# One pass over the k-tiles in the first FFN block, transposes moved into the next block, and FFN parts of 4, 4 and 3 blocks

## The chip, the core and the metric

The kernel runs on one core of a Trainium2 chip. The metric is the device time of one execution in microseconds (us); lower is better. Five engines run side by side, each taking its own instructions in order: TensorE (PE; its weight loads are listed as PEld), VectorE (DVE), ScalarE (ACT), GpSimd (POOL) and SyncE (SP), which here issues the transfers of the weights.

## What is computed

Two layers; in each a mixer of several attention-like heads, which the change does not touch, and then a SwiGLU block behind an RMS norm:

```python
def swiglu(h, w_gate, w_up, w_down):
    return (jax.nn.silu(h @ w_gate) * (h @ w_up)) @ w_down
...
for l in range(DEPTH):
    h = rms_norm(x, mix_norm_w[l])
    x = x + hybrid_mixer(h, ...)
    h = rms_norm(x, ffn_norm_w[l])
    x = x + swiglu(h, w_gate[l], w_up[l], w_down[l])
return rms_norm(x, final_norm_w)
```

x has 256 rows and 2048 columns, w_gate and w_up are 2048 x 5632, w_down is 5632 x 2048, all float32.

## The kernel before, in words

**Numbers.** Every float32 operand is split in a high part and a low part (`whi`, `wlo` of a weight; `hi`, `lo` of an activation). ACT makes the high part and DVE the low one, and a product is three matmuls: high by high, high by low, low by high. A weight comes from memory in units of 128 x 1024 (512 KB): `fetch` (L125) issues the transfer on SP into one of 3 buffers `raw`, `unit` (L140, L141) splits it into one of 4 buffer pairs `whi`, `wlo`. So DVE and ACT can be at most four units ahead of PE.

**Order.** The program is written through a framework that reorders instructions by its own model of the engines before it fixes the order on each queue; `tc.issue_after` (L70's log) only forbids a place before a given matmul. PSUM has eight banks: a pool of 4 (`dps`, tag "d", taken in rotation), `mg` with 2, `m0` and `m1` with one each (`mps`).

**FFN.** `ffn` works on blocks of 512 of the 5632 columns, 11 in all, and keeps x^T as 16 k-tiles `hl` (`hs`), high part and low part.

- The first block is `slow` (L923): all 16 k-tiles against w_gate into the two banks `pg`, then all 16 against w_up into `pu`, 96 matmuls each, on x^T that is not yet divided by the norm. Between the two, `norm.scale` gives the factor per row (`rstd`) and, through two small PE matmuls, the same along columns (`rb`). Behind both, `normalise` (L833) scales x^T in place, tile by tile: POOL adds high and low part (L841, `yn`), DVE multiplies by `rb` (L842), ACT and DVE split again into `hl` (L843, L844), POOL subtracts the two halves of the rows (L856, `dt`) and ACT and DVE split that (L829, L830, `sd`). Two pairs of tiles (3 and 4, 11 and 12) get three such combinations. A tile can only be overwritten when PE has read it for the last time.
- Every other block is `fast` (L893). With the sums in `sd` and combinations of the weights it computes gate and up together in 186 matmuls over seven PSUM banks `p1` to `p7` (`plain` 12 matmuls per k-tile, `quad` 21 per pair). At its end DVE and ACT put the banks together into `ga` (L915 to L921).
- Behind each block four PE transposes at a time (`hT`, 2 groups per block, L73) turn `ga`, and ACT and DVE split the result into `hid` (L951, L952), the left operand of the product with w_down.
- Blocks are gathered in parts, `FF_PARTS = (2, 2, 2, 2, 2, 1)`. After a part, `block_b` multiplies its `hid` with four column ranges of w_down (`dn`, two banks each), and `add_x` (L808) adds the result to x. In the last part `nxt.piece` starts on the following norm as each range is done; in the last layer this is `Final`, whose `last` (L310 and following) scales and stores one half of the rows after the other.

Of the kernel before, what the change touches and what calls it, by code (L numbers as in the profile page):

```python
# [20 lines left out]
P = 128  # L21
S = 256
# [1 line left out]
KT = D // P  # L24
DFF = 5632
FT = DFF // P
FF_PARTS = (2, 2, 2, 2, 2, 1)
PAIRS = (3, 11)
HM, HF, HG = 4, 8, 4
EPS = 1e-6  # L30
# [29 lines left out]
def tile_trunk(ctx: ExitStack, tc: tile.TileContext, x: bass.AP, wu: bass.AP, prm: bass.AP,  # L60
# [749 lines left out]
    def ffn(l, norm, nxt):  # L810
# [19 lines left out]
            dve.tensor_tensor(out=e[:, 1], in0=v, in1=f32(e[:, 0]), op=SUB)  # L830
            return e[:, 0], e[:, 1]

        def normalise(rb):  # L833

            free = [sd[i][:, j] for i in range(5) for j in range(4)]
            free = [v.rearrange("p (h x) -> p h x", h=2) if len(v.shape) == 2 else v for v in free]
            y = [None, None]
            for k in range(KT):
                hi, lo, hl = hs[k]
                y[k % 2] = yk = sp.tile([P, S], F32, tag="ac", name="yn", bufs=2)  # L840
                pool.tensor_tensor(out=yk, in0=f32(hi), in1=f32(lo), op=ADD)  # L841
                dve.tensor_tensor(out=yk, in0=yk, in1=rb, op=MUL)  # L842
                act.activation(out=hi, in_=yk, func=AF.Copy)  # L843
                dve.tensor_tensor(out=lo, in0=yk, in1=f32(hi), op=SUB)  # L844
                if k - 1 in PAIRS:
                    y0 = y[1 - k % 2]
                    st = sp.tile([P, 384], F32, tag="pt", name="st", bufs=2)
                    s1, s2, s4 = (st[:, i * P:(i + 1) * P] for i in range(3))
                    pool.tensor_tensor(out=s1, in0=y0[:, P:], in1=yk[:, P:], op=ADD)
                    pool.tensor_tensor(out=s2, in0=s1, in1=y0[:, :P], op=SUB)  # L850
                    pool.tensor_tensor(out=s4, in0=yk[:, :P], in1=s2, op=SUB)
                    for n, v in (("s1", s1), ("s2", s2), ("s4", s4)):
                        ops[n, k - 1] = hilo(free.pop(), v)
                else:
                    v = sp.tile([P, S], F32, tag="tz", name="dt", bufs=2)[:, :P]
                    pool.tensor_tensor(out=v, in0=yk[:, :P], in1=yk[:, P:], op=SUB)  # L856
                    ops["d", k] = hilo(free.pop(), v)

        def quad(c, k):

# [31 lines left out]

        def fast(c, first):  # L893

            ps = {3: dps("p3")}
            for i in ((1, 6, 7) if first else (2, 4, 5)):
                ps[i] = dps(f"p{i}")
            for i, tag in zip((2, 4, 5) if first else (6, 7, 1), ("mg", "mg", "m1")):
                ps[i] = mps(f"p{i}", tag)
            seen = set()  # L900
            for k in range(KT):
                if k - 1 in PAIRS:
                    continue
                for i, (ahi, alo), (whi, wlo) in quad(c, k) if k in PAIRS else plain(c, k):
                    end = k == KT - 1 or (i in (1, 6, 7) and k == PAIRS[-1])
                    pe.matmul(ps[i], ahi, whi, start=i not in seen, stop=False)
                    pe.matmul(ps[i], ahi, wlo, start=False, stop=False)
                    pe.matmul(ps[i], alo, whi, start=False, stop=end)
                    seen.add(i)
                if k == PAIRS[-1]:  # L910
                    act.copy(out=xs[:, 0], in_=ps[1])
                    dve.tensor_tensor(out=xs[:, 1], in0=ps[6], in1=xs[:, 0], op=ADD)
                    dve.tensor_tensor(out=ys[:, 0], in0=ps[7], in1=xs[:, 1], op=ADD)
# [7 lines left out]
                dve.tensor_tensor(out=ga[:, t], in0=ga[:, t], in1=ys[:, 1 - t], op=MUL)  # L921

        def slow(c):  # L923
            pg = [dps("pg") for t in range(2)]
            block_b(l, "gate", c, pg, hs, 0, KT, True, True)
            rstd, rb = norm.scale()
            for t in range(2):
                act.activation(out=ga[:, t], in_=pg[t], func=AF.Silu, scale=rstd[:, t:t + 1])
            pu = [dps("pu") for t in range(2)]
            block_b(l, "up", c, pu, hs, 0, KT, True, True)  # L930
            for t in range(2):
                dve.scalar_tensor_tensor(out=ga[:, t], in0=pu[t], scalar=rstd[:, t:t + 1], in1=ga[:, t],
                                         op0=MUL, op1=MUL)
            normalise(rb)

        for part, blocks in enumerate(FF_PARTS):
            nf = 4 * blocks
            fs = []
            for c in range(f0 * P, (f0 + nf) * P, 512):
                if c == 0:  # L940
                    slow(c)
                else:
                    fast(c, c == 512 or c == f0 * P)
                for q in range(0, 4, 2):
                    ps = mps("hT", "m0")
                    for i in range(2):
                        for t in range(2):
                            pe.transpose(ps[:, i * S + t * P:i * S + (t + 1) * P],
                                         ga[:, t, (q + i) * P:(q + i + 1) * P], ident)
                    hid = g4("hid", [2, 512], F32R, "gy")  # L950
                    act.copy(out=hid[:, 0], in_=ps)  # L951
                    dve.tensor_tensor(out=hid[:, 1], in0=ps, in1=f32(hid[:, 0]), op=SUB)  # L952
                    fs += [(hid[:, 0, i * S:(i + 1) * S], hid[:, 1, i * S:(i + 1) * S]) for i in range(2)]
            end = part == len(FF_PARTS) - 1
            for n in range(3 if end else 4):
                pst = [dps("dn") for t in range(2)]
                block_b(l, "down", n * 512, pst, fs, f0, nf, True, True)
                add_x(n, pst)
                if end:
                    nxt.piece(n)  # L960
# [97 lines left out]
```

## Time and profile before

| | |
|---|---|
| median of 3 runs | 2416.74 us (2416.14 to 2416.99) |
| the profiled execution, its own time | 2416.53 us |
| its span, first to last instruction | 2414.6 us |
| PE busy, share of the span | 98% |
| DVE, ACT, POOL busy | 70%, 50%, 12% |
| mean granted TensorE clock | 0.992 |
| first FFN block begins, layers 0 and 1 | 467.3 us, about 1663 us |
| HBM | 431.70 MB read, 180 GB/s over the span |

The 1.9 us between span and time lie around the profiled instructions. The profile puts busy time per engine, lists of waits and stretches of the execution side by side; a granted clock of 1.00 is 2.4 GHz for PE and 0.5 is 1.2 GHz.

### The profile page before, as it was taken

Reading aid. Unit: us, or ns where it says so; the run is one execution under the profiler, and the core shown is the slowest. Engines: PE = TensorE matmul, PEld = TensorE weight load, DVE = VectorE, ACT = ScalarE, POOL = GpSimd, SP = SyncE. Lnnn points to the kernel's source line nnn. Section 1 sums busy time; section 2 is a strip of 40 time slices with the busy share of each in tenths; the row PEclk is TensorE's granted clock in tenths of the full one; section 3 lists DMA queues with packets and bytes.
Section 4 is the critical chain, followed back from the end, with each engine's and each line's share of the span. In section 5 each row is a group of like instructions: output and inputs, shape, how many; then the busy total and the mean of one; then the engine's idle time right before and its main releaser. Section 6 shows DMA issues by size and latency. Waiting matters only on the chain.

```text
span 2414.6 us, 31866 instructions
## 1 busy us (share of the span) xinstructions
PE 2368.0 (98%) x11852; PEld 1995.4 (83%) x11852; DVE 1680.2 (70%) x2366; ACT 1212.0 (50%) x1783; POOL 278.3 (12%) x259
## 2 busy tenths in 40 slices
PE   9999999989999999999899999999999999999997
PEld 8888888867888888888798888888788888888886
DVE  5898655587676768576668976555866767676756
ACT  6754555554444444454466545555544444444443
POOL 0220000050101111010003000000501010111100
PEclk9999999999999999999999999999999999999998
DMA  6555455546565656665455554455465656565663
GB/s 218 167 174 175 138 166 176 176 166 198 175 210 191 200 185 200 191 198 183 151 169 175 175 163 152 155 186 192 148 200 191 201 169 213 192 196 186 203 203 114
DMA packets 120876, 435.89 MB, mean 181 GB/s; under 512 B 13584, under 2 KB 14480, under 8 KB 120720
## 3 DMA queue, kind: packets, MB, share of 16 engines
q1 hardware_dynamic: 120160, 432.70, 55.3%
q8 instruction: 93, 1.52, 0.3%
q10 hardware_dynamic: 560, 1.15, 0.1%
q14 instruction: 63, 0.52, 0.1%
HBM read 431.70 MB, written 2.10 MB: 180 GB/s over the span
## 4 chain that ended last, share of the span: by engine, by line
PE 88%; DVE 4%; issue 2%; ACT 2%; DMA 2%; POOL 1%; POOLq 0%; DVEq 0%; SPq 0%; ACTq 0%
PE p L70 31%; PE dn L70 19%; PE wo L70 7%; PE fq L70 4%; PE fk L70 4%; PE fv L70 4%; PE gkq L70 3%; PE mv L70 2%; DMA raw<-wu 2%; PE mq L70 2%; PE mk L70 2%; PE gvp L70 2%; PE gz L70 2%; PE pg L70 2%; DVE wlo L141 1%
## 5 line engine op out<-in xcount | busy, mean ns | idle before, releaser
L141 DVE TENSOR_TENSOR wlo<-raw,whi 128x1024 fp32r<-128x1024 f32 (+3 forms) x741 | 918.7, 1247 | 473.5 <-ACT whi L140 455.0
L140 ACT ACTIVATE whi<-raw 128x1024 fp32r<-128x1024 f32 (+3 forms) x741 | 775.8, 1053 | 772.2 <-PE dn L70 244.3
L70 PE MATMUL p<-whi,hl 128*128 128x512 f32 x1600 | 546.6, 391 | 1.0 <-ACT whi L140 1.0
L70 PE MATMUL dn<-whi,hid 128*128 128x512 f32 (+1 forms) x1440 | 444.3, 389 | 3.8 <-ACT hid L951 1.3
L70 PEld LDWEIGHTS p<-whi,hl 128*128 128x128 f32 x1600 | 301.3, 188 | 63.5 <-ACT whi L140 1.9
L70 PE MATMUL p<-wlo,hl 128*128 128x512 f32 x800 | 313.2, 392 | 7.1 <-DVE wlo L141 7.1
L70 PEld LDWEIGHTS dn<-whi,hid 128*128 128x128 f32 x1440 | 268.2, 189 | 60.0 <-ACT whi L140 3.0
L70 PE MATMUL dn<-wlo,hid 128*128 128x512 f32 (+1 forms) x720 | 277.2, 389 | 1.3 <-DVE wlo L141 1.3
L70 PE MATMUL p<-whi,sd 128*128 128x512 f32 x560 | 216.3, 391 | 0.0
L70 PEld LDWEIGHTS p<-wlo,hl 128*128 128x128 f32 x800 | 150.5, 188 | 41.0 <-DVE wlo L141 9.8
L874 POOL TENSOR_TENSOR rq<-rq 128x512 f32<-128x512 f32 x40 | 57.4, 1436 | 989.5 <-DVE rq L873 973.7
L70 PE MATMUL wo<-whi,yhl 128*128 128x512 f32 (+1 forms) x640 | 169.5, 351 | 0.0
L70 PEld LDWEIGHTS dn<-wlo,hid 128*128 128x128 f32 x720 | 136.5, 190 | 32.1 <-DVE wlo L141 5.2
L70 PEld LDWEIGHTS wo<-whi,yhl 128*128 128x128 f32 x640 | 112.6, 189 | 14.7
L70 PEld LDWEIGHTS p<-whi,sd 128*128 128x128 f32 x560 | 105.9, 189 | 21.6
L70 PE MATMUL wo<-wlo,yhl 128*128 128x512 f32 (+1 forms) x320 | 111.8, 349 | 0.0
L70 PE MATMUL p<-wlo,sd 128*128 128x512 f32 x280 | 109.8, 392 | 0.0
L878 ACT ACTIVATE th<-rq 128x1024 fp32r<-128x1024 f32 x80 | 84.0, 1050 | 43.8 <-POOL rq L876 27.8
L879 DVE TENSOR_TENSOR tl<-rq,th 128x1024 fp32r<-128x1024 f32 x80 | 99.8, 1248 | 3.5 <-ACT th L878 3.1
L876 POOL TENSOR_TENSOR rq<-rq 128x512 f32<-128x512 f32 x40 | 83.1, 2078 | 120.5 <-DVE rq L875 117.4
L871 DVE TENSOR_TENSOR wlo<-rq,whi 128x1024 fp32r<-128x1024 f32 x40 | 56.1, 1401 | 52.9 <-ACT whi L870 52.8
L870 ACT ACTIVATE whi<-rq 128x1024 fp32r<-128x1024 f32 x40 | 42.4, 1060 | 98.0 <-PE p L70 98.0
(362 smaller groups left out, 3527.2 us busy)
## 6 DMA issues: line engine op xcount, KB each, us to landing
raw<-wu SPq DMA_DIRECT2D x728, 512.0 KB, 4.2
rq<-wu SPq DMA_DIRECT2D x80, 512.0 KB, 4.2
raw<-wu SPq DMA_DIRECT2D x10, 420.0 KB, 3.0
xall<-x SPq DMA_DIRECT2D x3, 512.0 KB, 8.3
fw<-fnw SPq DMA_DIRECT2D x2, 512.0 KB, 6.8
out<-xall ACTq DMA_DIRECT2D x2, 512.0 KB, 3.3
out<-xall SPq DMA_DIRECT2D x2, 512.0 KB, 3.3
xall<-x SPq DMA_DIRECT2D x2, 256.0 KB, 4.4
```

Source lines behind the costliest of these rows:

```text
L70: self.log.append(nc.tensor.matmul(*a, **k).ins)
L140: act.activation(out=whi[:, c], in_=raw[:, c], func=AF.Copy)
L141: dve.tensor_tensor(out=wlo[:, c], in0=raw[:, c], in1=f32(whi[:, c]), op=SUB)
L870: act.activation(out=w1[0], in_=r1, func=AF.Copy)
L871: dve.tensor_tensor(out=w1[1], in0=r1, in1=f32(w1[0]), op=SUB)
L874: pool.tensor_tensor(out=b12, in0=b22, in1=b12, op=SUB)
L876: pool.tensor_tensor(out=b21, in0=b21, in1=b22, op=SUB)
L878: act.activation(out=hi, in_=v, func=AF.Copy)
L879: dve.tensor_tensor(out=lo, in0=v, in1=f32(hi), op=SUB)
```

## The change

- `slow` runs once over the 16 k-tiles, with units that hold 512 columns of gate and 512 of up for one k-tile: 12 matmuls per tile into `pg` and `pu` together, four "d" banks at once. `norm.scale` is called after the first tile, and `normalise(k, rb)` is called after each tile.
- The transposes of a block and the split into `hid` (now the function `hidden`) are put on a list, `pending`, and are issued inside the next `fast` block, behind k-tiles 5 and 7; those of a part's last block inside the first column range of the w_down product, behind its first and second four k-tiles.
- `FF_PARTS` is (4, 4, 3): three w_down stages per layer in place of six, with 16, 16 and 12 k-tiles each.
- `fast` takes its banks in another order and alternates its two bank assignments so that a part's last block has p1, p6, p7 and p3 in the "d" banks.

```diff
-FF_PARTS = (2, 2, 2, 2, 2, 1)
+FF_PARTS = (4, 4, 3)
...
-        def normalise(rb):
-
-            free = [sd[i][:, j] for i in range(5) for j in range(4)]
-            free = [v.rearrange("p (h x) -> p h x", h=2) if len(v.shape) == 2 else v for v in free]
-            y = [None, None]
-            for k in range(KT):
-                hi, lo, hl = hs[k]
...
+        free = [sd[i][:, j] for i in range(5) for j in range(4)]
+        yn = [None, None]
+
+        def normalise(k, rb):
+
+            hi, lo, hl = hs[k]
...
-            ps = {3: dps("p3")}
-            for i in ((1, 6, 7) if first else (2, 4, 5)):
-                ps[i] = dps(f"p{i}")
+            ps = {i: dps(f"p{i}") for i in ((1, 6, 7, 3) if first else (2, 4, 5, 3))}
...
+                if k in (5, 7) and pending:
+                    hidden()
...
-            pg = [dps("pg") for t in range(2)]
-            block_b(l, "gate", c, pg, hs, 0, KT, True, True)
-            rstd, rb = norm.scale()
+            pg, pu = ([dps(n) for t in range(2)] for n in ("pg", "pu"))
+            for k in range(KT):
+                whi, wlo = unit(("s", l, "ug", c, k, 1, 1024))
+                for j, pst in ((1, pg), (0, pu)):
+                    w = slice(j * 512, (j + 1) * 512)
+                    for t in range(2):
+                        ahi, alo = half(k, t)
+                        pe.matmul(pst[t], ahi, whi[:, w], start=(k == 0), stop=False)
+                        pe.matmul(pst[t], ahi, wlo[:, w], start=False, stop=False)
+                        pe.matmul(pst[t], alo, whi[:, w], start=False, stop=(k == KT - 1))
+                if k == 0:
+                    rstd, rb = norm.scale()
+                normalise(k, rb)
...
-            pu = [dps("pu") for t in range(2)]
-            block_b(l, "up", c, pu, hs, 0, KT, True, True)
...
-            normalise(rb)
+
+        pending = []
+
+        def hidden():
+
+            fs, q = pending.pop(0)
+            ps = mps("hT", "m0")
+            with tc.issue_after(pe.log[-1]):
+                for i in range(2):
+                    for t in range(2):
+                        pe.transpose(ps[:, i * S + t * P:i * S + (t + 1) * P],
+                                     ga[:, t, (q + i) * P:(q + i + 1) * P], ident)
+            hid = g4("hid", [2, 512], F32R, "gy")
+            act.copy(out=hid[:, 0], in_=ps)
+            dve.tensor_tensor(out=hid[:, 1], in0=ps, in1=f32(hid[:, 0]), op=SUB)
...
-                    fast(c, c == 512 or c == f0 * P)
-                for q in range(0, 4, 2):
...
+                    fast(c, (blocks - n) % 2 == 1)
+                pending += [(fs, 0), (fs, 2)]
...
-                block_b(l, "down", n * 512, pst, fs, f0, nf, True, True)
+                for j in range(0, nf, 4):
+                    block_b(l, "down", n * 512, pst, fs[j:j + 4], f0 + j, 4, j == 0, j == nf - 4)
+                    if n == 0 and j < 8:
+                        hidden()
```

**What moves, first place.** PE, end of the last part's last block in layer 0. `p_9672` and `p_9323` are the block's bank p3, `dn` the product with w_down. Before:

```order
L70 MATMUL p_9672<-whi,sd 128x512
L70 MATMUL p_9672<-wlo,sd 128x512
L70 MATMUL p_9672<-whi,sd 128x512
L73 MATMUL hT<-ident,ga 128x128 x4
L70 MATMUL dn<-whi,hid 128x512
L70 MATMUL dn<-wlo,hid 128x512
```

Now:

```order
L70 MATMUL p_9323<-whi,sd 128x512
L70 MATMUL p_9323<-wlo,sd 128x512
L70 MATMUL p_9323<-whi,sd 128x512
L70 MATMUL dn<-whi,hid 128x512
L70 MATMUL dn<-wlo,hid 128x512
L70 MATMUL dn<-whi,hid 128x512 x3
```

Before, the transposes of `ga` are the very next thing on PE. Now 48 matmuls of `dn`, on the `hid` of the part's first two blocks, stand between; behind the first two parts it is 52.

**Second place.** DVE, in the first block of layer 0, around k-tile 10. `wlo_5006` and `wlo_5033` are the units of k-tiles 10 and 11 (lines L840 to L855 of the changed kernel are `normalise`), `hl_4228` and `hl_4236` are k-tiles 5 and 6, `yn_4940` k-tile 7:

```order
L141 TENSOR_TENSOR wlo_5006<-raw_5003,whi_5005 128x1024
L830 TENSOR_TENSOR sd_4706<-st_4858,sd_4706 128x128
L841 TENSOR_TENSOR yn_4913<-yn_4913,rb_4743 128x256
L843 TENSOR_TENSOR hl_4228<-yn_4886,hl_4228 128x256
L830 TENSOR_TENSOR sd_4706<-dt_4891,sd_4706 128x128
L141 TENSOR_TENSOR wlo_5033<-raw_5030,whi_5032 128x1024
L843 TENSOR_TENSOR hl_4236<-yn_4913,hl_4236 128x256
L830 TENSOR_TENSOR sd_4705<-dt_4918,sd_4705 128x128
L841 TENSOR_TENSOR yn_4940<-yn_4940,rb_4743 128x256
```

Before, the first scaling (L842 there) stands on DVE behind the fourth of the eight up units, and six of the sixteen stand behind the evacuation of `pu`. Now one scaled tile goes with one unit, and the unit of tile k+5 stands ahead of the write of tile k.

**Third place.** DVE, end of the same block; `wlo_5203` and `wlo_5221` are the second and third unit of the next block, `pu_4716` the second bank of up:

```order
L141 TENSOR_TENSOR wlo_5203<-raw_5200,whi_5202 128x1024
L830 TENSOR_TENSOR sd_4703<-dt_5140,sd_4703 128x128
L841 TENSOR_TENSOR yn_5162<-yn_5162,rb_4743 128x256
L843 TENSOR_TENSOR hl_4688<-yn_5135,hl_4688 128x256
L141 TENSOR_TENSOR wlo_5221<-raw_5218,whi_5220 128x1024
L940 SCALAR_TENSOR_TENSOR ga_4712<-pu_4715,rstd_4737,ga_4712 128x512
L830 TENSOR_TENSOR sd_4703<-dt_5167,sd_4703 128x128
L940 SCALAR_TENSOR_TENSOR ga_4712<-pu_4716,rstd_4737,ga_4712 128x512
L843 TENSOR_TENSOR hl_4691<-yn_5162,hl_4691 128x256
```

The evacuation of `pu` (L940, L932 before) stands behind three units of the next block and all but the last write of x^T. The bank of `pu_4716` is the one that the next block's p3 takes; on PE the first matmul into p3 is the 16th of that block.

## Rows read from the trace of the kernel before

**Rows 1.** Stretches, PE's matmuls of L70 alone: length, busy (count), PEclk, DMA share, GB/s
```profile
705.00:820.00 115.00, 114.42 (x502) 1.00 0.59 188
467.30:1192.00 724.70, 703.09 (x3047) 0.99 0.58 187
1663.00:2388.00 725.00, 703.42 (x3040) 0.99 0.58 189
511.60:545.00 33.40, 25.87 (x101) 0.95 0.41 139
1707.00:1742.00 35.00, 28.51 (x108) 0.90 0.40 132
1170.00:1192.00 22.00, 14.19 (x55) 0.84 0.33 99
2366.00:2388.00 22.00, 13.90 (x51) 0.77 0.38 124
820.00:836.00 16.00, 15.28 (x66) 1.00 0.71 232
```
**Rows 2.** Stretches, PE's transposes (L73) alone
```profile
705.00:820.00 115.00, 1.79 (x12) 1.00 0.59 188
467.30:1192.00 724.70, 15.47 (x92) 0.99 0.58 187
```
**Rows 3.** Waits of PE: releaser, us in total, times, longest us
```profile
PE hT L73 <- DVE ga L921: 12.3, 6, 5.8
PE p L70 <- DVE wlo L141: 7.1, 5, 2.9
```
**Rows 4.** Timeline at the end of layer 0's last block: start us, us, engine, line
```profile
1175.29 0.39 PE L70 MATMUL p<-whi,sd 128*128 128x512 f32 x1
...
1180.08 1.29 DVE L921 TENSOR_TENSOR ga<-ga,pb 128x512 f32<-128x512 f32 x2
...
1181.52 1.09 PE L73 MATMUL hT<-ident,ga 128*128 128x128 f32 x4 [5.84 <-DVE ga L921]
...
1183.28 0.79 PE L70 MATMUL dn<-whi,hid 128*128 128x512 f32 x1 [0.67 <-ACT hid L951]
```
**Rows 5.** Stretches, all engines: length, PE, PEld, DVE, ACT, POOL busy (count), PEclk
```profile
491.60:512.00 20.40, 20.40 (x91) 16.89 (x91) 19.05 (x29) 12.29 (x25) 13.19 (x16) 1.00 0.54 179
512.00:540.00 28.00, 21.41 (x86) 15.29 (x85) 26.71 (x40) 14.61 (x29) 19.12 (x20) 0.94 0.35 116
```
**Rows 6.** Groups by line and shape: busy us, mean ns of one
```profile
L141 DVE TENSOR_TENSOR wlo<-raw,whi 128x1024 fp32r<-128x1024 f32 x727 | 906.2, 1253 | 458.4 <-ACT whi L140 439.9 <-PE fq L70 4.2 <-issue 3.8
L842 DVE TENSOR_TENSOR yn<-yn,rb 128x256 f32<-128x256 f32 x32 | 19.9, 632 | 2.1 <-POOL yn L841 2.1
L844 DVE TENSOR_TENSOR hl<-yn,hl 128x256 fp32r<-128x256 f32 x32 | 14.5, 464 | 1.0 <-ACT hl L843 1.0
L830 DVE TENSOR_TENSOR sd<-dt,sd 128x128 fp32r<-128x128 f32 x28 | 14.9, 542 | 0.1
L808 DVE TENSOR_TENSOR xall<-dn,xall 128x512 f32<-128x512 f32 x92 | 61.3, 687 | 11.3 <-PE dn L70 11.2
```
**Rows 7.** Timeline of DVE at the end of layer 0's first block
```profile
517.75 1.40 DVE L932 SCALAR_TENSOR_TENSOR ga<-pu,rstd,ga 128x512 f32<-128x512 f32 x2
```
**Rows 8.** Tile yn: line, engine, count, duration ns min/median/max
```profile
L841 POOL TENSOR_TENSOR yn<-hl x32: 734/786/1713, 420.8 to 1734.7; 128x256 f32<-128x256 f32 x32
L842 DVE TENSOR_TENSOR yn<-yn,rb x32: 410/416/1489, 493.8 to 1737.2; 128x256 f32<-128x256 f32 x32
L856 POOL TENSOR_TENSOR dt<-yn x28: 449/578/2788, 494.3 to 1737.7; 128x128 f32<-128x128 f32 x28
```
**Rows 9.** Transfers: issued by, count, KB each, median us to landing
```profile
rq<-wu SPq DMA_DIRECT2D x80, 512.0 KB, 4.2
```
**Rows 10.** Timeline of the last DVE steps of the kernel
```profile
2405.95 0.16 DVE L316 TENSOR_REDUCE fs<-fssq 128x1 f32<-128x5 f32 x1
...
2407.51 0.15 DVE L230 TENSOR_SCALAR frstd<-fs 128x1 f32<-128x1 f32 x1
```

More of the change, by code (lines that the diff above doesn't have):

```diff
@@ L831, in hilo @@
             return e[:, 0], e[:, 1]
-        def normalise(rb):
-            free = [sd[i][:, j] for i in range(5) for j in range(4)]
-            free = [v.rearrange("p (h x) -> p h x", h=2) if len(v.shape) == 2 else v for v in free]
-            y = [None, None]
-            for k in range(KT):
-                hi, lo, hl = hs[k]
[L840 to L857, printed above, removed]
@@ new lines, in ffn @@
+        free = [sd[i][:, j] for i in range(5) for j in range(4)]
+        yn = [None, None]
+        def normalise(k, rb):
+            hi, lo, hl = hs[k]
+            yn[k % 2] = yk = sp.tile([P, S], F32, tag="ac", name="yn", bufs=2)
+            pool.tensor_tensor(out=yk, in0=f32(hi), in1=f32(lo), op=ADD)
+            dve.tensor_tensor(out=yk, in0=yk, in1=rb, op=MUL)
+            act.activation(out=hi, in_=yk, func=AF.Copy)
+            dve.tensor_tensor(out=lo, in0=yk, in1=f32(hi), op=SUB)
+            if k - 1 in PAIRS:
+                y0 = yn[1 - k % 2]
+                st = sp.tile([P, 384], F32, tag="pt", name="st", bufs=2)
+                s1, s2, s4 = (st[:, i * P:(i + 1) * P] for i in range(3))
+                pool.tensor_tensor(out=s1, in0=y0[:, P:], in1=yk[:, P:], op=ADD)
+                pool.tensor_tensor(out=s2, in0=s1, in1=y0[:, :P], op=SUB)
+                pool.tensor_tensor(out=s4, in0=yk[:, :P], in1=s2, op=SUB)
+                for n, v in (("s1", s1), ("s2", s2), ("s4", s4)):
+                    ops[n, k - 1] = hilo(free.pop(), v)
+            else:
+                v = sp.tile([P, S], F32, tag="tz", name="dt", bufs=2)[:, :P]
+                pool.tensor_tensor(out=v, in0=yk[:, :P], in1=yk[:, P:], op=SUB)
+                ops["d", k] = hilo(free.pop(), v)
@@ L933, in slow @@
                                          op0=MUL, op1=MUL)
-            normalise(rb)
+        pending = []
[10 more added lines that the diff above has]
+            dve.tensor_tensor(out=hid[:, 1], in0=ps, in1=f32(hid[:, 0]), op=SUB)
+            fs += [(hid[:, 0, i * S:(i + 1) * S], hid[:, 1, i * S:(i + 1) * S]) for i in range(2)]
         for part, blocks in enumerate(FF_PARTS):
@@ L938, in ffn @@
             fs = []
-            for c in range(f0 * P, (f0 + nf) * P, 512):
+            for n in range(blocks):
+                c = (f0 + 4 * n) * P
                 if c == 0:
@@ L942, in ffn @@
                 else:
-                    fast(c, c == 512 or c == f0 * P)
-                for q in range(0, 4, 2):
[L945 to L953, printed above, removed]
+                    fast(c, (blocks - n) % 2 == 1)
+                pending += [(fs, 0), (fs, 2)]
             end = part == len(FF_PARTS) - 1
```

## The prediction

> **What bounds the kernel now.** I read the stretches of PE's own work first, because PE is busy nearly everywhere: in the FFN of layer 0 its matmuls of L70 cover 703.09 of 724.70 us [rows 1]. A busy PE says little about its pace, so I count. In a stretch inside one FFN part, 705 to 820 us, there are 502 matmuls and 12 transposes [rows 1, 2]. A count takes in one instruction that reaches over the edge, so 501; a transpose streams 128 columns and is taken as half a matmul, a choice that moves the sums below by some 2 us. That makes 115.00 / 507 = 0.2268 us per matmul. Everything in the FFN beyond this pace is lost time: in layer 0 724.70 - 0.2268 x (3046 + 46) = 23.4 us, in layer 1 725.00 - 0.2268 x (3039 + 46) = 25.3 us [rows 1, 2], together 48.7.
>
> Where it is lost, by the same working, with eight transposes in each stretch: behind the first block 33.40 - 0.2268 x 104 = 9.8 us, and 9.8 again in layer 1; around the last block's end 8.8 and 9.8 [rows 1]. These four places are 38.2 of the 48.7. The remaining 10.5 lie at the other ten ends of blocks before a down stage; the one at 820 to 836 us is typical, 16.00 - 0.2268 x 67 = 0.8 [rows 1].
>
> The waits of PE name the causes. At the last block's end PE waits for `ga`, 5.8 us at the longest [rows 3]: PE finishes p3 at 1175.3, DVE needs until 1181.4 to put the banks together, and nothing else may run on PE meanwhile [rows 4]. Behind the first block PE waits for `wlo` [rows 3], because DVE has half of `normalise` still to do: it is busy 26.71 of 28.00 us between 512 and 540 [rows 5]. In both places the clock adds to it: the granted share is 0.95 and 0.90 behind the first block, 0.84 and 0.77 around the last block's end, against 1.00 in the undisturbed stretch [rows 1]; the matmuls behind such a wait run partly at 1.2 GHz.
>
> **The change, part by part.** The profiled execution took 2416.5 us, 0.2 under the median of the runs, and the sum is made against it.
>
> Work on PE: the same number of matmuls (192 in the first block, 186 in each other, the same w_down products) and of transposes, so nothing, either way. Transfers: the same units of 512 KB. On SP the first two `rq` transfers now stand behind the fifth unit of the next block; one lands after 4.2 us [rows 9], and PE needs its first product some 36 matmuls, 8 us, into that block. Nothing.
>
> Parts of 4, 4 and 3: 24 of 46 additions of `dn` to x per layer go, 48 x 0.687 = 33 us of DVE [rows 6]. They lie beside the w_down product and DVE itself mostly waits for PE before them (11.2 us) [rows 6]. Nothing on the path.
>
> Last block's end: the transposes now have 48 matmuls of other blocks ahead of them, 10.9 us. DVE's chain for `ga` took 6.1 us from the last p3 matmul [rows 4]; the new order puts one more `wlo` in it, 1.25 us [rows 6], which makes 7.3. So the wait goes, and with it the slow clock behind it: 8.8 + 9.8 = 18.6 us gained. If the cover failed, what lacks in 10.9 us would come back as a wait, six times.
>
> Other block ends: half of the down stages go, and the transposes inside a block stand 15 us behind the end of the block before. The 10.5 us go, apart from what the six ends now cost: nothing at best, 0.8 each at worst [rows 1]; the order puts the banks of p1 and p6, free early, under the first `dn`, so I take the middle, 0.4, together 2.4.
>
> First block: `normalise` gets DVE's idle time of the gate half. The question is whether DVE is done in time. In 491.6 to 512, where both run side by side, 29 DVE instructions took 19.05 us [rows 5], 0.657 each; a k-tile now has 4.25 of them (unit, scaling, split, and 20 splits of `sd` over 16 tiles), so 2.79 us, against 12 x 0.2268 = 2.72 on PE. The first scaling needs `rb`, whose matmuls stand behind 33 others and four transposes, 7.9 us, and then ACT's copy: 8.6 us, with the units to tile 5 done. From there to the evacuation of the second `pu` bank DVE has ten tiles with their units (27.9), six without (2.79 - 1.25 = 1.54 each, 9.2), three units of the next block (3.8) and the two evacuations, 1.4 [rows 7]: 42.3, so 50.9 us after the start. PE is through the block after 0.2268 x 195 = 44.2 and wants that bank for p3 15 matmuls later, at 47.6. What is late next is this bank: 3.3 us per layer. The bounds are no wait at all (`yn` took 0.41 us where POOL left it alone [rows 8], 0.63 on average [rows 6]) and the 9.8 us that were lost here before. I take 3.3, 6.6 in all, as it comes from the stretch where the same mixture ran.
>
> Kernel's end: the last half of the rows waited for DVE, which was scaling the first half; its reduction was done at 2406.1 and the next step began at 2407.5 [rows 10]. Now 36 matmuls of half width stand between the two halves instead of 12, time for the first half's steps. 1.4 us gained.
>
> Sum: 48.7 + 1.4 = 50.1 that can go; 2.4 + 6.6 = 9.0 that stay. 2416.5 - 41.1 = 2375.4.
>
> **Rivals.** *DVE stays the bound behind the first block.* Then the 9.8 us per layer only move from `wlo` to the bank of p3 and the time is 2416.5 - 50.1 + 2.4 + 19.6 = 2388.4. For it: DVE's 2.79 us per tile is no less than PE's 2.72. Against it: the order keeps the units four to five tiles ahead, and DVE loses no time in the gate half any more.
>
> *DVE and POOL exclude each other.* With a tile's DVE work at 2.79 less the 0.22 by which `yn` is over its minimum, and POOL's at its minima, 0.73 + 0.45 [rows 8], a tile would take 3.75 us: 37.5 + 6 x 2.5 + 5.2 = 57.7 us behind 8.6, a wait of 18.7 per layer, and 2406. Against it: at that price 6.8 tiles take 25.5 us, and the 20.40 us from 491.6 held them without a loss on PE [rows 5]. The Trainium skill ("SBUF — State Buffer", Who interferes with whom) says that a DVE instruction with two SBUF inputs contends with a GpSimd instruction that reads SBUF, and calls the shared ports an exclusive lock; it speaks against spreading POOL's work over the units. By that rule taken whole it would be 2406; the trace shows the contention (0.41 to 1.49 us for one `yn` [rows 8]) but not the whole of it.
>
> *Slower: the write of x^T holds up the units.* `normalise` can only write a tile when PE has read it. If PE's next unit stood right behind that write on DVE, every k-tile would cost the write and the unit more, 0.46 + 1.25 = 1.7 us [rows 6]; 32 tiles make 54, against 47.7 gained, so 2423. It decides from 1.5 us per tile. Against it: in the order the unit of tile k+5 stands ahead of the write of tile k.
>
> *It does not do what it says*: the transposes could wait in their new places as long as before, which would leave some 2416. The order gives them 10.9 us and 15 us of other work, so this is remote.
>
> **Numbers.** The forecast 0.84, the first rival 0.10, the lock 0.02, slower 0.03, no change 0.01. The likeliest time is 2375. Its lower bound is 2366.4, everything lost given back, less 1 for the counting; upwards I go to the first rival, 2388. Faster by more than 0.2% (5 us, about what a measurement of this kernel can tell from no change): 0.96; within: 0.01; slower: 0.03.
>
> **What would show it.** In the profile after: `hT` no longer among the longest waits of PE; behind the first block a wait of p3 or `wlo` of about 3 us in place of 9.8; granted clock 1.00 at both places; some 0.4 us at each of three part ends; the last scalar steps of the second half right behind the reduction. A wait of PE on `wlo` within the first block, spread over its k-tiles, would make the prediction wrong.

## The result and the profile after

The changed kernel takes 2380.35 us (median of four runs, 2379.96 to 2383.44) against 2416.86 for the kernel before beside it: a ratio of 0.9851, 95% interval 0.9834 to 0.9868. The profiled execution took 2379.96 us, with a span of 2378.1; the span of before was 2414.6, so 36.5 us went, where the prediction had 41.1.

Where they went shows in the same stretches as in [rows 1, 2]: PE's matmuls of L70 (length, busy, count, granted clock, DMA share, GB/s), first the two FFNs up to their last column range (by the prediction's count 3090 and 3081 matmuls, about the 3092 and 3085 of [rows 1, 2]), then the stretch behind each layer's first block, the same that is used for every kernel below, and last a part of layer 1's last column range.

```profile
467.30:1175.00 707.70, 699.29 (x3037) 1.00 0.57 192
1646.50:2352.00 705.50, 696.67 (x3036) 1.00 0.58 194
505.00:550.00 45.00, 41.34 (x168) 0.96 0.57 195
1683.00:1735.00 52.00, 47.23 (x200) 1.00 0.61 206
2354.00:2370.00 16.00, 16.00 (x136) 1.00 0.11 40
```

And the transposes of L73 in the two FFN stretches and the two behind the first block:

```profile
467.30:1175.00 707.70, 16.48 (x108) 1.00 0.57 192
1646.50:2352.00 705.50, 13.93 (x92) 1.00 0.58 194
505.00:550.00 45.00, 1.20 (x8) 0.96 0.57 195
1683.00:1735.00 52.00, 1.20 (x8) 1.00 0.61 206
```

By the prediction's working (0.2268 us per matmul, a transpose half of one, one off each count) the FFN of layer 0 loses 707.70 - 0.2268 x (3036 + 54) = 6.9 us and that of layer 1 705.50 - 0.2268 x (3035 + 46) = 6.7: 13.6 in place of 48.7. Nearly all of it lies behind the first block: 45.00 - 0.2268 x (167 + 4) = 6.2 and 52.00 - 0.2268 x (199 + 4) = 6.0. For all ends of parts and of last blocks together 1.4 us are left.

PE's waits say the same. `hT`, 12.3 us in [rows 3], is no longer among them; the wait of `p` for `wlo` is, with 5.6 us in place of 7.1 (releaser, us in total, times, longest us):

```profile
PE p L70 <- DVE wlo L141: 5.6, 4, 1.6
PE p L70 <- ACT ga L938: 0.7, 2, 0.4
```

Two of its four places follow each other at the start of layer 0's second block (timeline of PE: start us, us, what it waited for; the first row is the first block's first matmul):

```profile
467.03 0.40 PE L70 MATMUL pg<-whi,hl 128*128 128x512 f32 x1
...
512.00 0.39 PE L70 MATMUL p<-whi,hl 128*128 128x512 f32 x1
514.00 0.50 PE L70 MATMUL p<-wlo,hl 128*128 128x512 f32 x1 [1.61 <-DVE wlo L141]
...
517.59 0.50 PE L70 MATMUL p<-wlo,hl 128*128 128x512 f32 x1 [1.17 <-DVE wlo L141]
...
519.37 0.51 PE L70 MATMUL p<-whi,sd 128*128 128x512 f32 x1 [0.34 <-ACT ga L938]
```

PE has the high part of the block's first unit, and DVE finishes the low part at 513.95, because it was still scaling tiles of the first block. The matmul at 519.37 is the first into p3, the 16th of the block. It starts before both evacuations of `pu` (the second, at 520.59, stands below), and it was released by ACT's step on `pg` (L938). So p3 takes a bank of `pg` here, not that of `pu_4716`, as the part on the change has it.

DVE's timeline, from the first scaling to the second evacuation of `pu`:

```profile
475.80 1.22 DVE L141 TENSOR_TENSOR wlo<-raw,whi 128x1024 fp32r<-128x1024 f32 x1
476.93 0.75 DVE L841 TENSOR_TENSOR yn<-yn,rb 128x256 f32<-128x256 f32 x2
...
511.11 0.82 DVE L830 TENSOR_TENSOR sd<-st,sd 128x128 fp32r<-128x128 f32 x1
511.86 0.95 DVE L841 TENSOR_TENSOR yn<-yn,rb 128x256 f32<-128x256 f32 x1
512.74 1.21 DVE L141 TENSOR_TENSOR wlo<-raw,whi 128x1024 fp32r<-128x1024 f32 x1
...
520.59 0.74 DVE L940 SCALAR_TENSOR_TENSOR ga<-pu,rstd,ga 128x512 f32<-128x512 f32 x1
```

POOL at the same moments:

```profile
510.87 1.66 POOL L840 TENSOR_TENSOR yn<-hl 128x256 f32<-128x256 f32 x2
512.89 1.37 POOL L855 TENSOR_TENSOR dt<-yn 128x128 f32<-128x128 f32 x1 [0.36 <-DVE yn L841]
```

The scaling that starts at 511.86 takes 0.95 us and ends 0.28 us behind POOL's two additions (510.87 + 1.66 = 512.53); POOL's difference that starts at 512.89, beside DVE's `wlo`, takes 1.37 and ends 0.31 behind it (512.74 + 1.21 = 513.95). The two engines hold each other up here. Whether that is what is left behind the first block, the runs further down have to show.

At the kernel's end the scalar step of the second half now begins 0.03 us behind its reduction, where it began 1.40 behind it [rows 10]:

```profile
2371.47 0.16 DVE L316 TENSOR_REDUCE fs<-fssq 128x1 f32<-128x5 f32 x1
2371.66 0.15 DVE L230 TENSOR_SCALAR frstd<-fs 128x1 f32<-128x1 f32 x1
```

From that reduction to the end of the span it is 2378.1 - 2371.5 = 6.6 us, before 2414.6 - 2406.0 = 8.6: 2.0 gained.

### The profile page after: what moved, and what is told of

It reads as the page before. It is cut to its first block, busy times and chain, and to the rows that moved or that the text cites. A ratio compares the mean times of both kernels' runs of the same rounds, so it can differ in the third digit from the quotient of the medians.

```text
span 2378.1 us, 32020 instructions
## 1 busy us (share of the span) xinstructions
PE 2355.5 (99%) x11948; PEld 1995.9 (84%) x11948; DVE 1668.3 (70%) x2318; ACT 1213.9 (51%) x1783; POOL 285.6 (12%) x259
## 4 chain that ended last, share of the span: by engine, by line
PE 91%; DVE 3%; ACT 2%; issue 1%; POOL 1%; DMA 1%; POOLq 0%; DVEq 0%; ACTq 0%; SPq 0%
PE p L70 34%; PE dn L70 20%; PE wo L70 7%; PE fq L70 4%; PE fk L70 4%; PE fv L70 4%; PE gkq L70 3%; PE mq L70 2%; PE mk L70 2%; PE gvp L70 2%; PE gz L70 2%; PE mv L70 2%; ACT whi L140 1%; DVE wlo L141 1%; PE hT L73 1%
## 5 line engine op out<-in xcount | busy, mean ns | idle before, releaser
L70 PE MATMUL p<-whi,hl 128*128 128x512 f32 x1600 | 548.3, 392 | 0.4 <-ACT whi L869 0.4
L70 PE MATMUL dn<-whi,hid 128*128 128x512 f32 (+1 forms) x1504 | 440.8, 376 | 0.0
L70 PEld LDWEIGHTS p<-whi,hl 128*128 128x128 f32 x1600 | 300.2, 188 | 62.2 <-ACT whi L869 0.9
L70 PE MATMUL p<-wlo,hl 128*128 128x512 f32 x800 | 313.0, 391 | 5.6 <-DVE wlo L141 5.6
L70 PEld LDWEIGHTS dn<-whi,hid 128*128 128x128 f32 x1504 | 275.8, 188 | 50.5
L70 PE MATMUL dn<-wlo,hid 128*128 128x512 f32 (+1 forms) x752 | 281.8, 376 | 0.0
L70 PE MATMUL p<-whi,sd 128*128 128x512 f32 x560 | 216.8, 391 | 0.7 <-ACT ga L938 0.7
L70 PEld LDWEIGHTS p<-wlo,hl 128*128 128x128 f32 x800 | 150.4, 188 | 40.1 <-DVE wlo L141 9.4
L873 POOL TENSOR_TENSOR rq<-rq 128x512 f32<-128x512 f32 x40 | 66.1, 1652 | 921.5 <-DVE rq L872 921.5
L70 PE MATMUL wo<-whi,yhl 128*128 128x512 f32 (+1 forms) x640 | 169.4, 350 | 0.0
L70 PEld LDWEIGHTS dn<-wlo,hid 128*128 128x128 f32 x752 | 141.5, 188 | 25.6
L70 PEld LDWEIGHTS p<-whi,sd 128*128 128x128 f32 x560 | 105.5, 188 | 23.3 <-ACT ga L938 1.6
L70 PEld LDWEIGHTS wo<-whi,yhl 128*128 128x128 f32 x640 | 112.6, 189 | 14.8
L878 DVE TENSOR_TENSOR tl<-rq,th 128x1024 fp32r<-128x1024 f32 x80 | 109.4, 1368 | 17.9 <-ACT th L877 16.9
L70 PE MATMUL wo<-wlo,yhl 128*128 128x512 f32 (+1 forms) x320 | 111.7, 349 | 0.0
L70 PE MATMUL p<-wlo,sd 128*128 128x512 f32 x280 | 109.4, 391 | 0.0
L875 POOL TENSOR_TENSOR rq<-rq 128x512 f32<-128x512 f32 x40 | 84.0, 2099 | 116.1 <-DVE rq L874 94.2
L70 PE MATMUL p<-th,sd 128*128 128x512 f32 x240 | 89.4, 390 | 0.6 <-ACT th L877 0.6
L870 DVE TENSOR_TENSOR wlo<-rq,whi 128x1024 fp32r<-128x1024 f32 x40 | 63.7, 1594 | 29.6 <-ACT whi L869 29.4
```

Source lines behind the costliest of these rows:

```text
L70: self.log.append(nc.tensor.matmul(*a, **k).ins)
L870: dve.tensor_tensor(out=w1[1], in0=r1, in1=f32(w1[0]), op=SUB)
L873: pool.tensor_tensor(out=b12, in0=b22, in1=b12, op=SUB)
L875: pool.tensor_tensor(out=b21, in0=b21, in1=b22, op=SUB)
L878: dve.tensor_tensor(out=lo, in0=v, in1=f32(hi), op=SUB)
```

## The parts of the change, one at a time

Four kernels took the change apart; all ran on one chip beside the kernel before (2415.33 us).

**Part sizes alone** (`x1_parts`): the kernel before with the new parts and the alternating banks; transposes and first block stay in the program as they were.

```diff
-FF_PARTS = (2, 2, 2, 2, 2, 1)
+FF_PARTS = (4, 4, 3)
...
-                    fast(c, c == 512 or c == f0 * P)
+                    fast(c, (blocks - n) % 2 == 1)
```

> The kernel before with parts of 4, 4 and 3 blocks and alternating banks alone; the first block in two passes, the transposes in the program's old place behind each block. My theory: the w_down products of other blocks are all the cover that the last block's transposes need, and the scheduler moves them there by itself. The two waits of 5.8 us with their slow clock (18.6 us) and most of the 10.5 us at other block ends go, 1.3 us come for 96 more matmuls of half width, 2 us go at the kernel's end, and 9.8 us per layer behind the first block stay: 2390 us (2387 to 2394). Rival: the transposes must be put into the next block by hand; then most of the wait before hT stays and the time is 2405 us or more.

Measured: 2387.25 us, ratio 0.9885 (0.9869 to 0.9902). This edit is worth 28.1 of the 36.5 us. Its rows: the two stretches of PE behind the first block, and the wait of `hT`.

```profile
505.00:550.00 45.00, 37.52 (x153) 0.96 0.40 135
1683.00:1735.00 52.00, 46.30 (x183) 0.90 0.44 142
...
PE hT L73 <- DVE ga L932: 1.7, 2, 0.9
```

Behind the first block it loses 45.00 - 0.2268 x 156 = 9.6 and 9.8 us, as much as before, and the waits of `hT` at the last block's end are gone, 1.7 us being left behind the first block. So the scheduler itself puts other work ahead of a block's transposes once fewer blocks end a part.

**First block in two passes** (`x2_two_pass`): the change with the old order of the first block, gate, then up, then all 16 scalings.

```diff
-            pg, pu = ([dps(n) for t in range(2)] for n in ("pg", "pu"))
...
+            block_b(l, "gate", c, pg, hs, 0, KT, True, True)
+            rstd, rb = norm.scale()
...
+            block_b(l, "up", c, pu, hs, 0, KT, True, True)
...
+            for k in range(KT):
+                normalise(k, rb)
```

> The changed kernel with the first block in two passes and all of the scaling behind them, as before. Theory: only the loss behind the first block comes back, 9.8 us per layer in place of the 6.2 measured in the changed kernel: 2387 us (2385 to 2390), with granted clock below 1.00 behind the first block in both layers. Rival: the transposes that now stay out of that stretch were a good part of its loss; then it stays near 6 us per layer and the time is 2380 to 2382 us.

Measured: 2385.91 us, ratio 0.988 (0.9865 to 0.9895). It differs from the part sizes alone by the transposes that are placed by hand and by the order of the banks (worth nothing, `x4_banks` below), and those two times lie 1.3 us apart with overlapping intervals: placing them is worth 1 us or nothing.

**One pass alone** (`x3_one_pass`): the kernel before with `slow` and `normalise(k, rb)` of the change, in parts of two blocks.

```diff
-            normalise(rb)
...
+                if k == 0:
+                    rstd, rb = norm.scale()
+                normalise(k, rb)
```

> The kernel before with the first block in one pass alone (parts of 2, transposes behind each block). Theory: the loss behind the first block falls from 9.8 to about 6.2 us per layer and nothing else moves: 2409.5 us (2407 to 2412), and the waits of hT for ga, 5.8 us, stay. Rival: DVE's 9.8 us are only moved into the first block or to the transposes behind it; then 2415 us or more.

Measured: 2406.01 us, ratio 0.9961 (0.9947 to 0.9976): 9.3 us, a little more than expected (the time lies 1 us under the stated range). Behind the first block it loses 5.8 and 5.7 us by the same count, and the wait at the last block's end stays:

```profile
505.00:550.00 45.00, 40.78 (x170) 1.00 0.55 193
1683.00:1735.00 52.00, 47.57 (x201) 1.00 0.55 189
...
PE hT L73 <- DVE ga L920: 12.1, 5, 5.8
```

The two halves add up: 28.1 + 9.3 = 37.4 against 36.5 for the whole.

**Banks in the old order** (`x4_banks`):

```diff
-            ps = {i: dps(f"p{i}") for i in ((1, 6, 7, 3) if first else (2, 4, 5, 3))}
+            ps = {3: dps("p3")}
+            for i in ((1, 6, 7) if first else (2, 4, 5)):
+                ps[i] = dps(f"p{i}")
...
-                    fast(c, (blocks - n) % 2 == 1)
+                    fast(c, (part == 0 and n % 2 == 1) or (part > 0 and n % 2 == 0))
```

> The changed kernel with p3 first in the bank order, as before, and a part's first block (not its last) with p1, p6, p7 in the d banks. Theory: the bank order is worth the 0.3 us at the passage from a block to its down stage, at one or two of the three part ends per layer: 2381 us (2380 to 2383). Rival: without the new order a block's p3 or the first dn waits for the evacuation of the bank before it, 2 us or more at ten places: 2390 us or more.

Measured: 2380.01 us, ratio 0.9853 (0.9839 to 0.9868). The order of the banks is worth nothing that can be measured, and the loss behind the first block stays at 6.2 and 6.0 us: the bank of p3 does not set it.

## What holds PE up behind the first block

What stays is 6 us per layer there. Three kernels take something from that stretch, each of the change; the fourth to eighth move it. The kernel before took 2416.10 to 2417.04 us beside them, so a microsecond between two of these kernels says nothing.

**Without POOL's addition** (`y1_no_add`):

```diff
-            pool.tensor_tensor(out=yk, in0=f32(hi), in1=f32(lo), op=ADD)
-            dve.tensor_tensor(out=yk, in0=yk, in1=rb, op=MUL)
+            dve.tensor_tensor(out=yk, in0=f32(hi), in1=rb, op=MUL)
```

> Left out: POOL's addition of the low part of x^T, so that DVE scales the high part alone. Question: why do about 6 us per layer remain behind the first block. Theory 'contention' (DVE's small instructions stretch while POOL runs beside them): 16 of POOL's 36 to 40 instructions go, DVE's k-tile shortens by 0.2 to 0.3 us, and the loss behind the first block falls from 6.2 to 2 to 3 us per layer; time 2372 (2370 to 2374). Theory 'amount' (DVE simply has 2.7 us of its own work per k-tile, whoever runs beside it): nothing changes, 2379 to 2381. Theory 'chain' (POOL, ACT and DVE hand a tile on, and DVE waits for its turn): one link goes, the first scaling starts as late as now because it waits for the broadcast of rstd, so 2377 to 2380.

Measured: 2379.01 us, ratio 0.9844 (0.9829 to 0.9859); 5.1 and 6.6 us lost. No gain that can be told from none (the intervals overlap), so the number that "contention" gave was wrong here. The trace shows why: its timeline for one k-tile, DVE, POOL and ACT.

```profile
510.54 1.23 DVE L141 TENSOR_TENSOR wlo<-raw,whi 128x1024 fp32r<-128x1024 f32 x1
510.62 1.46 POOL L854 TENSOR_TENSOR dt<-yn 128x128 f32<-128x128 f32 x1 [1.72 <-ACT whi L140]
512.12 0.31 ACT L829 ACTIVATE sd<-dt 128x128 fp32r<-128x128 f32 x1 [1.61 <-POOL dt L854]
512.46 0.30 DVE L830 TENSOR_TENSOR sd<-dt,sd 128x128 fp32r<-128x128 f32 x1 [0.70 <-ACT sd L829]
...
513.23 0.42 DVE L840 TENSOR_TENSOR yn<-hl,rb 128x256 f32<-128x256 f32 x1
513.72 1.23 DVE L141 TENSOR_TENSOR wlo<-raw,whi 128x1024 fp32r<-128x1024 f32 x1
```

The scheduler had put `wlo` right behind the scaling, where POOL's difference wants to run. POOL's 128 columns, 0.45 us at best, take 1.46 and end 0.31 us behind `wlo`; ACT copies only then, and DVE stands 0.70 us for the copy. The tile takes 513.72 - 510.54 = 3.18 us against 2.72 on PE. DVE's last steps then come late in another place, and PE waits mainly for a bank that ACT has yet to empty:

```profile
PE p L70 <- ACT ga L937: 5.0, 2, 2.5
```

**Without the low part of the sums** (`y2_no_sdlo`):

```diff
-            dve.tensor_tensor(out=e[:, 1], in0=v, in1=f32(e[:, 0]), op=SUB)
+            act.activation(out=e[:, 1], in_=v, func=AF.Copy, scale=0.0)
```

> Left out: the low parts of the 20 sums and differences, which ACT fills with zeros in place of DVE's subtraction. DVE loses 20 x 0.54 = 10.9 us of work per layer behind the first block, ACT gains about 6. Theories 'amount' and 'contention' (DVE is the bound there, whatever makes it so): the loss of 6.2 us per layer goes to 0 to 1, time 2368 to 2370. Theory 'chain' (DVE waits for ACT's copies and the late start, its amount does not matter): the loss stays over 4 us per layer, 2376 to 2382, since ACT has more to do.

Measured: 2376.53 us, ratio 0.9836 (0.9821 to 0.9851); 4.6 and 4.6 us lost. Between 478 and 514 us DVE is busy 27.17 of 36 us, where it was 33.50 in the change (stretch of all engines: PE, PEld, DVE, ACT, POOL), and still late:

```profile
478.00:514.00 36.00, 35.52 (x157) 29.10 (x156) 27.17 (x38) 22.91 (x60) 25.41 (x31) 1.00 0.51 167
```

A quarter of DVE's time is free and most of the loss stays, as "chain" had it: DVE's amount of work is not what decides in this kernel. DVE now stands and waits for POOL's additions (between 476.9 and 521.3 us; 1.9 us in the change):

```profile
DVE yn L841 <- POOL yn L840: 4.8, 6, 1.6
```

ACT has more to do here too, so this kernel alone does not clear DVE's amount; the next one leaves the amounts of both engines as they are.

**Without POOL's work** (`y3_no_pool`):

```diff
-            pool.tensor_tensor(out=yk, in0=f32(hi), in1=f32(lo), op=ADD)
-            dve.tensor_tensor(out=yk, in0=yk, in1=rb, op=MUL)
+            dve.tensor_tensor(out=yk, in0=f32(hi), in1=rb, op=MUL)
...
-                pool.tensor_tensor(out=s1, in0=y0[:, P:], in1=yk[:, P:], op=ADD)
-                pool.tensor_tensor(out=s2, in0=s1, in1=y0[:, :P], op=SUB)
-                pool.tensor_tensor(out=s4, in0=yk[:, :P], in1=s2, op=SUB)
+                s1, s2, s4 = y0[:, P:], y0[:, :P], yk[:, :P]
...
-                pool.tensor_tensor(out=v, in0=yk[:, :P], in1=yk[:, P:], op=SUB)
-                ops["d", k] = hilo(free.pop(), v)
+                ops["d", k] = hilo(free.pop(), yk[:, :P])
```

> Left out: all of POOL's work behind the first block (the addition of the low part of x^T and the 20 sums and differences of halves); ACT and DVE split slices of the scaled tile instead, so their amounts stay as in the change. 'Contention with its hand-offs' (DVE's and POOL's instructions on SBUF wait for each other, and the engines hand a tile on in a fixed order): DVE's scaling, low part and split take 0.41, 0.41 and 0.28 us without exception, a k-tile costs DVE 1.21 + 0.41 + 0.41 + 1.25 x 0.28 = 2.4 us against 2.72 on PE, and of the loss of 6.2 us per layer 0 to 2 are left: 2368 to 2372. 'Amount' (DVE's own work is too much, whoever runs beside it): 5 to 6 us per layer stay, 2378 to 2381. That POOL's addition alone was not the cause (2379 without it) speaks neither for nor against: its differences still ran beside wlo there, 1.47 us each.

Measured: 2368.76 us, ratio 0.9801 (0.9787 to 0.9814), 11.6 us less than the change. The loss behind the first block is gone (PE's stretches of L70 as above: 45.00 - 0.2268 x 199 and 52.00 - 0.2268 x 229, -0.1 and 0.1 us). DVE has as many instructions per tile as in the change, and none stretches (tile `sd` and tile `yn`: count, duration min/median/max):

```profile
505.00:550.00 45.00, 44.62 (x196) 36.33 (x196) 1.00 0.59 209
1683.00:1735.00 52.00, 51.61 (x226) 42.11 (x226) 1.00 0.58 203
...
L830 DVE TENSOR_TENSOR sd<-yn,sd x40: 282/285/289, 479.6 to 1682.8; 128x128 fp32r<-128x128 f32 x40
L840 DVE TENSOR_TENSOR yn<-hl,rb x32: 418/420/426, 477.4 to 1681.2; 128x256 f32<-128x256 f32 x32
L842 DVE TENSOR_TENSOR hl<-yn,hl x32: 415/420/426, 479.3 to 1687.8; 128x256 fp32r<-128x256 f32 x32
```

The same groups in the change, with POOL beside them:

```profile
L830 DVE TENSOR_TENSOR sd<-dt,sd x28: 276/413/831, 479.9 to 1699.6; 128x128 fp32r<-128x128 f32 x28
L841 DVE TENSOR_TENSOR yn<-yn,rb x32: 409/416/959, 476.9 to 1696.9; 128x256 f32<-128x256 f32 x32
L843 DVE TENSOR_TENSOR hl<-yn,hl x32: 407/414/685, 479.0 to 1700.5; 128x256 fp32r<-128x256 f32 x32
L855 POOL TENSOR_TENSOR dt<-yn x28: 450/578/1444, 477.4 to 1697.4; 128x128 f32<-128x128 f32 x28
```

So POOL's share in the scaling is the cause of what is left behind the first block. It can act in two ways: the instructions of DVE and POOL hold each other up, or DVE stands and waits until POOL hands a tile on. Taking POOL away takes both, but the traces tell them apart for DVE. Its time from the first scaling to the end of the second evacuation of `pu` in layer 0 (length, busy, count), in the change and without POOL, and its waits for POOL in the change:

```profile
476.93:521.33 44.40, 41.57 (x68) 0.98 0.51 173
477.45:514.14 36.69, 32.61 (x68) 1.00 0.65 224
...
DVE yn L841 <- POOL yn L840: 1.9, 3, 0.6
```

The same 68 instructions are busy 9.0 us longer beside POOL. Idle time is 2.8 us with POOL and 4.1 without, so in the change DVE is late by its lengthened instructions, and not by waiting. Which of POOL's instructions do it is not separated: with the additions alone left out, the differences fell beside `wlo`.

**Late tiles, held back by PE's instructions** (`z2_late12`, `z2_late9`): the scaling of the last four or seven tiles is called in the next block, behind `tc.issue_after` of a matmul.

```diff
+                for i in range(2 if k in PAIRS else 1):
+                    if rest:
+                        with tc.issue_after(pe.log[-1]):
+                            normalise(*rest.pop(0))
...
-                normalise(k, rb)
+                if k < LATE:
+                    normalise(k, rb)
+            rest.extend((k, rb) for k in range(LATE, KT))
```

> Nothing left out: the scaling and splitting of the last four k-tiles moves into the next block, one tile behind each of its first k-tiles. Some 6 to 7 us of DVE work per layer leave the stretch ahead of the second scalar_tensor_tensor of the first block. 'Amount' and 'contention': the loss behind the first block falls from 6.2 to 0 to 2 us per layer, time 2368 to 2372; the next block has room, DVE is needed there for about 30 of its 42 us. 'Chain': 2377 or more. A risk that both share: the four tiles meet the first pair of k-tiles of the next block, where DVE has 5 us of splitting for 4.8 us on PE; then 2 to 3 us per layer come back as a wait for wlo or tl, 2374.

> As before, with the last seven k-tiles moved instead of four. 11 us of DVE work per layer leave the stretch ahead of the second scalar_tensor_tensor and meet the next block's units and its first pair. 'Amount' and 'contention': the loss behind the first block goes, but 3 to 6 us per layer come back inside the first half of the next block as waits for wlo, tl or sd: 2372 to 2378, later than with four tiles. If DVE's amount is not the bound: the same as with four tiles, within 1 us.

Measured: 2380.49 us, ratio 0.9852 (0.9838 to 0.9867), with four tiles, and 2377.43, ratio 0.9839 (0.9823 to 0.9856), with seven; 6.4 and 6.2, and 4.9 and 4.8 us lost. With seven tiles DVE's timeline still has the scalings ahead of the next block's first `wlo`, only some splits moved: such a bound holds back the instructions of the engine that it names, and here that was PE. These two did not test what they were made for.

**Late tiles, held back by DVE's instructions** (`z3_late11`, `z3_late9`): the same, but DVE's scaling now stands behind the low half of the next block's unit.

```diff
-            dve.tensor_tensor(out=wlo[:, c], in0=raw[:, c], in1=f32(whi[:, c]), op=SUB)
+            marks[0] = dve.tensor_tensor(out=wlo[:, c], in0=raw[:, c], in1=f32(whi[:, c]), op=SUB).ins
...
+                        with tc.issue_after(marks[0]):
+                            normalise(*rest.pop(0))
```

> Nothing left out: DVE's part of the last five k-tiles (scaling, low part, splits) now really stands behind the units of the next block in DVE's order, one tile behind the low half of each; with the deferral by PE's instructions DVE's order had kept the tiles ahead of the next block's first unit. Four units of DVE's order stand closer together there. Whatever makes DVE late behind the first block, some 6 to 8 us of it now stand behind what PE needs first: the loss falls from 6.2 to 1 to 3 us per layer, time 2370 to 2375. If the chain through ACT and the banks holds PE up, not DVE's place in the order: 2378 to 2381. If the tiles come back as waits at the first pair of k-tiles of the next block: 2375 to 2379.

> The same with the last seven k-tiles, two more units of the next block ahead of them. DVE then has some idle time late in the first block (it waits for free unit buffers), and more behind it: loss 0 to 3 us per layer, 2369 to 2376; better than with five tiles only if the first unit of the next block is still late there.

Measured: 2374.66 us, ratio 0.9825 (0.9812 to 0.9838), with five late tiles; 2376.34, ratio 0.9834 (0.982 to 0.9847), with seven. The first is the fastest kernel here that computes everything: 5.7 us under the change by the medians, with intervals of the ratio that just overlap. It loses 6.2 and 2.6 us, the other 3.0 and 2.3, in other places. With five late tiles the wait for the next block's `wlo` is no longer in the list, and a wait at its first pair of k-tiles (`th`, from `quad`) has taken its place (lines of these kernels are numbered one or more higher):

```profile
PE p L71 <- ACT th L879: 3.0, 2, 2.4
```

**Late tiles away from the pairs** (`z4_places`): six late tiles, only beside k-tiles without a `quad`.

```diff
-LATE = 11
+LATE, PLACES = 10, (0, 1, 5, 6, 7, 8)
...
-                for i in range(2 if k in PAIRS else 1):
-                    if rest:
+                if k in PLACES and rest:
```

> Nothing left out: the last six k-tiles are scaled in the next block as in the two runs before, but only beside its k-tiles 0, 1, 5, 6, 7 and 8, so that none stands in DVE's order between the splits of the first pair (k-tiles 3 and 4), where five late tiles left a wait of up to 2.4 us for th, and none is left for the second pair (11 and 12), where seven late tiles left waits. With the cause held (DVE and POOL in each other's way, too much for the first block, not for both blocks together) the loss behind the first block and at the first pair falls to 0 to 2 us per layer: 2369 to 2373. If th at the first pair is late for another reason (the transfers of rq or the order behind the next block's first units), 1 to 2.5 us per layer stay there: 2373 to 2376.

Measured: 2380.17 us, ratio 0.9849 (0.9836 to 0.9863): a miss. 4.9 and 4.6 us are lost in the same stretches, and the wait for `th` has grown:

```profile
PE p L71 <- ACT th L879: 4.4, 5, 1.3
```

Why the pairs' splits come later with these places was not followed further.

## Why the prediction held, and where its steps failed

| term | predicted | the trace |
|---|---|---|
| last blocks' ends and part ends, what stays | 2.4 us | 1.4 us, with everything else in the FFNs outside the next line |
| behind the first block, what stays | 6.6 us | 12.2 us |
| kernel's end | 1.4 us gained | 2.0 gained |
| work on PE | 0 | 1.1 to 1.3 us more |

By these rows 48.7 - 13.6 = 35.1, with 2.0 gained and 1.1 to 1.3 spent, make 35.8 to 36.0 of the 36.5 us; the rest is within a count of one per stretch. The forecast is 4.6 us under the profiled time: the first block and the work on PE cost 5.6 and some 1.2 us more than it had, and the ends of blocks and the kernel's end gave back 1.0 and 0.6 more. That these partly cancel is luck.

- **Bound.** The two kinds of seam that the counting named were the right ones: the first edit of those above took 28.1 us, the one pass 9.3, as places that hardly touch each other.
- **Ends of blocks.** Right in size. The reason was half right: that 48 matmuls cover the 7.3 us of DVE was enough, but no hand-placed transpose was needed for it, and the bank order that was named for the 0.4 us per end has no part in it (`x4_banks`).
- **First block: the step that failed.** The term was mis-sized, 6.6 us forecast and 12.2 measured, and the wait that it was worked out from is not there. "The question is whether DVE is done in time" was right, and so was the count: 13 units of `wlo` run from the first scaling to the second evacuation. DVE starts 1.3 us later than worked out (476.93 - 467.03 = 9.9 us after the block's start, not 8.6): `rb` is there after 8.8 us, but one more `wlo` of 1.22 us stands ahead of the first scaling. DVE then needs 521.33 - 476.93 = 44.4 us, not 42.3. Together it is done at 54.3 us instead of 50.9. But no matmul of p3 waits for that evacuation: p3 has another bank and waits 0.3 to 0.4 us for ACT. PE meets DVE earlier, at the low half of the next block's first two units (1.6 and 1.2 us in the list), which stand in DVE's order behind the scalings. With the measured times the prediction's own path would give 54.3 - 47.6 = 6.7 us per layer, near the 6.1 measured; that is luck.
- **The units taken as there.** That DVE has the next block's units ready rested on its order ("the order keeps the units four to five tiles ahead") and was not priced. PE is through the first block after 512.00 - 467.03 = 45.0 us, and the first of these units is split after 513.95 - 467.03 = 46.9.
- **Signs.** `hT` left the list, and `wlo` and p3 stand there with 5.6 + 0.7 us, about 3 per layer, as named. The granted clock of 1.00 came in layer 1 and not in layer 0 (0.96). These 6.3 us are half of the 12.2 by count: the list leaves out a part of each wait (it has 1.61 of the 1.77 us lost ahead of 514.00), the slow matmuls of layer 0 and waits under other names.
- **Range.** Its lower bound, 2366.4, is 2416.5 - 50.1; the 1 us "for the counting" is not in it.
- **Work on PE.** That "the same number of matmuls" makes "nothing, either way" was wrong. The last part now has 12 k-tiles in place of 4, and its last column range is multiplied in halves of 256 columns. The groups of `dn` with the high part of the weight, two of each product's three matmuls (shape, count | busy us, mean ns), before:

```profile
L70 PE MATMUL dn<-whi,hid 128*128 128x512 f32 x1376 | 432.6, 394 | 3.8 <-ACT hid L951 1.3 <-DVE ga L915 1.1 <-ACT whi L140 1.1
L70 PE MATMUL dn<-whi,hid 128*128 128x256 f32 x64 | 12.1, 284 | 0.0
```

and after:

```profile
L70 PE MATMUL dn<-whi,hid 128*128 128x512 f32 x1312 | 405.5, 390 | 0.0
L70 PE MATMUL dn<-whi,hid 128*128 128x256 f32 x192 | 35.6, 284 | 0.0
```

  With the third matmul, 1.5 x 64 = 96 of 512 columns went and 1.5 x 128 = 192 of 256 came. In the stretch 2354 to 2370 above, 135 of the latter take 16.00 us, 0.119 each, a little more than half of 0.2268: 192 x 0.119 - 96 x 0.2268 = 1.1 us. By their starts, 15 of them from 2368.30 to 2370.10, they take 0.12, which makes 1.3.
- **Rivals.** That DVE stays the bound behind the first block (2388) came nearest: 12.2 of the 19.6 us that it wanted stay, though as a wait for `wlo`. The slower one did not appear: within the first block PE runs at its pace, but for one place of some 0.3 us at 508.8. The exclusion of DVE and POOL was put at 2406 and taken as remote. As a mechanism it is what the runs show; as a price it was too high, since it added whole durations: 57.7 us were reckoned from the first scaling to the second evacuation, and the trace has 44.4, against 36.7 without POOL. The Trainium skill ("SBUF — State Buffer", Who interferes with whom) calls the ports that the two engines share an exclusive lock. The trace agrees in that the held-up instruction ends behind the other engine's, but only by 0.28 and 0.31 us, less than the 0.41 and 0.45 that it takes alone.

## What to carry to other kernels

Count a stage's loss by instructions and pace, stage by stage, before and after an edit: it gave the size of four terms here to within a microsecond or so, where the busy share of PE (98 and 99%) shows nothing. When work is spread over a loop so that it hides, price the instructions by what stands beside them in that loop and look at what the in-order queue puts behind them; here the supply of the next block's weights, not the last result, was what came late. Before placing work by hand, try the size of the parts alone: the larger ones, with the scheduler's own order, gave 28 of 36 us.

## What was not expected of the hardware

- POOL's subtraction of 128 columns takes 0.45 us alone and 1.46 us when DVE's subtraction of 1024 columns starts 0.08 us ahead of it; DVE's scaling of 256 columns takes 0.41 and, behind two of POOL's additions, 0.95. Without POOL all 104 such instructions of DVE (scaling, low part, split) lie within 11 ns of their kind.
- The same waits of PE, 1.6, 1.2 and 0.3 us, came with a granted clock below 1 in one layer (0.96 in the stretch from 505) and not in the other (1.00 in the stretch from 1683). The lower level of 1.2 GHz followed the waits in layer 0, where matmuls start 0.43 us apart from 520.11 to 523.10, and not in layer 1; the loss was 6.2 and 6.0 us all the same.
